# Gated-attention block: token halves of the MLP as even and odd chunks, their sums made in attention, both MLP stages laid out anew

## The chip, the cores and the metric

The kernel runs on one core of a Trainium2 chip, in one launch. The metric is device microseconds, the median of three timed runs. Beside them stands one execution taken by the hardware profiler, whose trace gives every row that is quoted here.

## The reference, cut to what matters

The input x is 2048 tokens of 1024 float32 values; a context of 256 tokens goes through the attention only. One layer is computed: a gated linear attention with a scan in both directions, then an MLP with squared ReLU, then a final RMS norm.

```python
a = modulate(rmsnorm(x, norm1_g), shift1, scale1)
o = gla_mixer(a_ctx, a)                        # scan over chunks, gate, output projection w_o
h = x + gate1 * o                              # h_d
h2 = modulate(rmsnorm(h, norm2_g), shift2, scale2)   # (2048, 1024)
m = square(relu(h2 @ mlp_w1)) @ mlp_w2         # 1024 -> 4096 -> 1024
out = rmsnorm(h + gate2 * m, final_g)
```

## The kernel before, in words

Matmuls run on float32r operands. So that the result keeps float32's precision, each operand is split into a high part (a ScalarE cast) and a low part (a subtraction), and `mm3` (lines 80 to 83) makes three matmuls of every one: high x high, high x low, low x high. A split is always such a pair, a cast and then a subtraction.

The kernel has four stages. (1) Up to about 889 us: projections and the scan (untouched by the change). (2) Up to about 1130 us, attention's second stage (lines 644 to 783): a loop over 16 chunks of 128 tokens. `front(ch)` finishes the scan's output, `turn_o` transposes it, `back(ch)` multiplies by w_o (48 matmuls of 512 columns), adds x, stores h to `h_d` and makes the normed rows hn. `turn(ch, hn)` (lines 747 to 770), called within the next chunk's `back`, transposes hn in eight blocks into two PSUM tiles, applies scale and shift while evicting them (half on ScalarE, L759, half on VectorE, L762) into `a2` (512 features x 128 tokens, float32), and stores that to `h2_d` (L764). For three of the four quarters of block 0 it also makes the split operands at once, into tiles of the pool `hold` (16 tiles of 4 KB a partition).

(3) The first MLP stage (lines 793 to 1001) computes square(relu(h2 @ w1)) in two blocks of 1024 tokens. It uses seven products in place of eight for a 2 x 2 blocked product (Strassen's scheme in Winograd's form). The token side has the quarters B11, B12, B21, B22 (first index: half of the 1024 features; second: half of the block's tokens, 512 each) and the sums T1 = B12 - B11, T2 = B22 - T1, T3 = B22 - B12, T4 = B21 - T2. The weight side has, for each of 16 pairs p of 128-column pieces of w1, A11 to A22 and the sums S1 to S4. The products are

```python
PROD = {1: ("a", "A11", "B11"), 5: ("b", "S1", "T1"), 6: ("a", "S2", "T2"), 2: ("c", "A12", "B21"),
        7: ("a", "S3", "T3"), 3: ("b", "S4", "B22"), 4: ("a", "A22", "T4")}
```

Each is 12 matmuls (4 k x `mm3`) of 512 columns. The letter names the PSUM accumulator, of which pool a has three banks, b three, c two. Products 1, 6, 7 and 4 of a pair add up in one bank; after product 1 its value is copied out (L967), after 6 too (L976), after 7 added to z22 (L981), after 4 evicted through ReLU (L985); bank b is copied after 5 (L973) and read after 3 (L978), bank c after 2 (L969). A matmul that goes on in a bank waits until the value was read. `order()` gives the order of products: for p >= 3 it is 1, 5, 6, 2, 7, 3, 4.

`load_h` (lines 815 to 850) loads a block's eight raw tiles from `h2_d` (L823), makes the sums (L804) and splits them (L808, L809, the subtractions on VectorE and GpSimd in turn) into the pool `m_t` of 18 tiles. For block 1 it is called at the last pair of block 0. `load_w1(p)` loads two raw tiles into `hold` (L864), makes S1 to S4 on VectorE and splits all seven operands (L857 the casts, L858 the subtractions: S1, S2, S4 and A11 on VectorE, S3, A12 and A22 on GpSimd). `sums_w2` makes sums of w2 for the last stage and stores them to `wt_d`. The seven hidden operands of each pair go to `hs_d` (L995).

(4) The second MLP stage (lines 1008 to 1124) does the same with w2: seven products, each over 16 pairs and two groups of 256 tokens; it loads `hs` tiles (L1025) and w2 tiles and splits them (L1030, L1031, L1040, L1041), and a product's result goes into `acc` and at the end to `out`. Output rows of token half 0 are the first 512 of a block, of half 1 the other 512.

What sets the order: the program is written down in order, and a planner fills each engine's queue from it, taking what it holds ready, in the order of priority. `tc.high_priority(offset=n)` gives instructions a priority as if they stood n instructions earlier. Each queue then runs in its order, and an instruction waits for the semaphores of what it needs. SyncE's queue (SP) issues nearly all DMAs. A pool with `reuse_waits="tile"` lets a new tile wait only for those older tiles that lay on its place; pools are stacked, so the order in which a stage opens its pools decides which tiles of the stage before lie there.

Of the kernel before, what the change touches and what calls it, by code (L numbers as in the profile page):

```python
# [8 lines left out]
F32 = mybir.dt.float32  # L9
# [4 lines left out]
ALU = mybir.AluOpType  # L14
# [23 lines left out]
def kernel(  # L38
# [34 lines left out]
    h2_d = dram.tile([P, ND, T], F32, name="h2_d")  # L73
# [561 lines left out]

    h2 = {}

    def h2_block(key):
        h2[key] = tuple(held([2, 512], F32R, "h2", 2) for _ in range(2))
# [4 lines left out]
    with ExitStack() as sb:  # L644
        wk = sb.enter_context(tc.tile_pool(name="b_wk", bufs=2, reuse_waits="tile"))
        wkx = sb.enter_context(tc.tile_pool(name="b_wkx", bufs=2, reuse_waits="tile"))
        wq = sb.enter_context(tc.tile_pool(name="b_q", bufs=2, reuse_waits="tile"))
        wk2 = sb.enter_context(tc.tile_pool(name="b_wk2", bufs=2, reuse_waits="tile"))
# [66 lines left out]
        def back(ch, onh, onl, hn_prev=None, mid=None, o_next=None):  # L715
            if ch == 0:
                h2_block((0, 0))
                h2_block((1, 0))
            elif ch == 4:
                h2_block((1, 1))  # L720
# [25 lines left out]

        def turn(ch, hn):
            for k4 in range(2):
# [4 lines left out]
                ks = slice(4 * k4, 4 * k4 + 4)  # L753
                t0 = (ch % 4) * P
                a2 = wk2.tile([P, 4, P], F32, tag="a2", name="a2", bufs=3)
# [8 lines left out]
                nc.sync.dma_start(h2_d[:, ks, ch * P:(ch + 1) * P], a2)  # L764
                if ch < MB // P and (k4, ch // 4) in h2:
                    for i in range(2):
                        dh, dl = (t_[i][:, :, t0:t0 + P] for t_ in h2[k4, ch // 4])
                        a_ = a2[:, 2 * i:2 * i + 2]
                        nc.scalar.copy(dh, a_)
                        nc.gpsimd.tensor_sub(dl, a_, dh.bitcast(F32))  # L770
# [8 lines left out]
        on = turn_o(nxt)  # L779
        for ch in range(1, NCH):  # L780
            nxt = front(ch + 1) if ch + 1 < NCH else None
            hn, on = back(ch, *on, hn, o_next=nxt)
# [10 lines left out]
    with ExitStack() as sm:  # L793
        tp = sm.enter_context(tc.tile_pool(name="m_t", bufs=18, reuse_waits="tile"))
        wp = sm.enter_context(tc.tile_pool(name="m_w", bufs=10, reuse_waits="tile"))
        cp = sm.enter_context(tc.tile_pool(name="m_c", bufs=2, reuse_waits="tile"))
        ev = sm.enter_context(tc.tile_pool(name="m_ev", bufs=12, reuse_waits="tile"))
# [3 lines left out]
        NK = ND // 2  # L801
# [4 lines left out]
        def split_h(src, alloc, eng):  # L806
            hi, lo = alloc(), alloc()
            nc.scalar.copy(hi, src)  # L808
            eng.tensor_sub(lo, src, hi.bitcast(F32))  # L809
            return hi, lo  # L810

        def t_tile(dtype=F32R, name="ht"):
            return tp.tile([P, 2, 512], dtype, tag="t", name=name)

        def load_h(b):
            r = {}
            for key in ((0, 0), (1, 0), (0, 1), (1, 1)):
                kh, th = key
                for j in range(2):
                    r[key, j] = t_tile(F32, "hraw")  # L820
                    k0 = NK * kh + 2 * j
                    t0 = b * MB + 512 * th
                    nc.sync.dma_start(r[key, j], h2_d[:, k0:k0 + 2, t0:t0 + 512])  # L823
            ops = {}

            def put(name, srcs, alloc, engs):
                hl = [split_h(s_, alloc, e_) for s_, e_ in zip(srcs, engs)]
                ops[name] = ([x_[0] for x_ in hl], [x_[1] for x_ in hl])
# [18 lines left out]
            if b > 0:  # L847
                put("B22", [r[(1, 1), j] for j in range(2)], hb, engs)
# [304 lines left out]
```

## Time and profile before

| | us |
|---|---|
| median of three runs | 2455.28 (2452.62 to 2456.47) |
| profiled execution | 2452.73 |
| its span, first to last instruction | 2451.0 |
| TensorE busy | 2303.0 |
| VectorE busy | 1580.3 |
| ScalarE busy | 1235.9 |
| GpSimd busy | 688.7 |

The span is what lies between the first and the last instruction of the profiled execution; the time of that execution has 1.7 us more. Busy time of an engine is the sum of its instructions without their overlap; matmuls overlap by their pipeline, so that a row's mean duration (390 ns) is longer than the spacing of two matmuls. Where a helper such as `mm3`, `tt` or a split makes every operation, the line number is the helper's and the tile names tell operations apart: pa, pb, pc are the first MLP stage's accumulators, yp attention's and the last stage's, pt the transposes, w1h and w1l split weights, ht or h split token operands, z and hs hidden values. Digits at the end of names are left out, so that `h2_d` stands as h_d.

### The profile page before, as it was taken

Reading aid. Unit: us, or ns where it says so; the run is one execution under the profiler, and the core shown is the slowest. Engines: PE = TensorE matmul, PEld = TensorE weight load, DVE = VectorE, ACT = ScalarE, POOL = GpSimd, SP = SyncE. Lnnn points to the kernel's source line nnn. Section 1 sums busy time; section 2 is a strip of 40 time slices with the busy share of each in tenths; the row PEclk is TensorE's granted clock in tenths of the full one; section 3 lists DMA queues with packets and bytes.
Section 4 is the critical chain, followed back from the end, with each engine's and each line's share of the span. In section 5 each row is a group of like instructions: output and inputs, shape, how many; then the busy total and the mean of one; then the engine's idle time right before and its main releaser. Section 6 shows DMA issues by size and latency. Waiting matters only on the chain. (4 is left out here: it accounts for less than half of the span.)

```text
span 2451.0 us, 36499 instructions
## 1 busy us (share of the span) xinstructions
PE 2303.0 (94%) x13250; PEld 2004.7 (82%) x13250; DVE 1580.3 (64%) x2287; ACT 1235.9 (50%) x2223; POOL 688.7 (28%) x765
## 2 busy tenths in 40 slices
PE   6899999999999989997899996999989999999998
PEld 4899999999999967785787884777768888888886
DVE  7855776676766677676866558665655448745484
ACT  6544544554555546554555554545554435444351
POOL 2334234434334434211322224222211113201021
PEclk8999999999999999998999998999999999999999
DMA  8223453444533277876466665666658657756572
GB/s 273 82 94 104 149 176 125 162 158 129 164 124 113 76 239 245 267 225 210 147 198 208 194 205 157 206 202 189 193 195 303 213 191 255 260 189 214 182 261 75
DMA packets 367934, 450.55 MB, mean 184 GB/s; under 512 B 22876, under 2 KB 273828, under 8 KB 367752
## 3 DMA queue, kind: packets, MB, share of 16 engines
q1 hardware_dynamic: 365080, 439.84, 54.8%
q0 software_dynamic: 2416, 8.07, 1.0%
q8 instruction: 104, 1.70, 0.3%
q14 instruction: 78, 0.64, 0.1%
q10 hardware_dynamic: 256, 0.29, 0.0%
HBM read 314.95 MB, written 133.17 MB: 183 GB/s over the span
## 5 line engine op out<-in xcount | busy, mean ns | idle before, releaser
L81 PE MATMUL yp<-w2h,hsh 128*128 128x512 f32 x896 | 349.7, 390 | 8.4 <-ACT hsh L1040 8.4
L83 PE MATMUL yp<-w2h,hsl 128*128 128x512 f32 x896 | 349.7, 390 | 0.1
L82 PE MATMUL yp<-w2l,hsh 128*128 128x512 f32 x896 | 349.5, 390 | 0.0
L342 POOL TENSOR_TENSOR wl<-wraw,wh 128x1024 fp32r<-128x1024 f32 x95 | 234.9, 2492 | 240.9 <-ACT wh L340 224.7
L858 POOL TENSOR_TENSOR w1l<-w1r,w1h 128x512 fp32r<-128x512 f32 x96 | 150.1, 1567 | 435.5 <-ACT w1h L857 290.3
L1041 DVE TENSOR_TENSOR hsl<-hsr,hsh 128x1024 fp32r<-128x1024 f32 x112 | 141.3, 1265 | 178.2 <-ACT hsh L1040 178.1
L1040 ACT CAST hsh<-hsr 128x1024 fp32r<-128x1024 f32 x112 | 117.7, 1052 | 204.1 <-PE yp L82 189.5
L1031 POOL TENSOR_TENSOR w2l<-w2r,w2h 128x512 fp32r<-128x512 f32 x56 | 81.5, 1456 | 462.0 <-ACT w2h L1030 358.4
L81 PEld LDWEIGHTS yp<-w2h,hsh 128*128 128x128 f32 x896 | 168.8, 188 | 43.9 <-ACT hsh L1040 8.9
L83 PEld LDWEIGHTS yp<-w2h,hsl 128*128 128x128 f32 x896 | 168.7, 188 | 35.9 <-DVE hsl L1041 0.8
L82 PEld LDWEIGHTS yp<-w2l,hsh 128*128 128x128 f32 x896 | 168.8, 188 | 35.1
L1030 ACT CAST w2h<-w2r 128x512 fp32r<-128x512 f32 x224 | 137.6, 620 | 93.1 <-PE yp L83 62.2
L81 PE MATMUL pa<-ht,w1h 128*128 128x512 f32 x384 | 154.3, 402 | 13.7 <-DVE z L981 7.4
L81 PE MATMUL vps<-wh,ah 128*128 128x256 f32 x576 | 165.1, 287 | 0.0
L82 PE MATMUL vps<-wl,ah 128*128 128x256 f32 x576 | 164.6, 286 | 0.0
L83 PE MATMUL vps<-wh,al 128*128 128x256 f32 x576 | 164.4, 285 | 0.0
L81 PE MATMUL kqps<-ah,wh 128*128 128x256 f32 x544 | 155.8, 286 | 0.0
L82 PE MATMUL kqps<-al,wh 128*128 128x256 f32 x544 | 154.8, 285 | 0.0
L83 PE MATMUL kqps<-ah,wl 128*128 128x256 f32 x544 | 154.1, 283 | 0.3 <-DVE wl L342 0.3
L82 PE MATMUL pa<-ht,w1h 128*128 128x512 f32 x384 | 150.4, 392 | 1.7 <-POOL ht L809 1.7
L83 PE MATMUL pa<-ht,w1l 128*128 128x512 f32 x384 | 149.7, 391 | 0.0
L82 PE MATMUL rps<-wl,ah 128*128 128x256 f32 x512 | 145.0, 283 | 0.0
(1278 smaller groups left out, 6498.1 us busy)
## 6 DMA issues: line engine op xcount, KB each, us to landing
hsr<-hs_d SPq DMA_DIRECT2D x112, 512.0 KB, 4.0
w2r<-in_mlp_w_dram SPq DMA_DIRECT2D x160, 256.0 KB, 4.1
wraw<-in_gla_w_in_dram SPq DMA_DIRECT2D x64, 512.0 KB, 3.8
w1r<-in_mlp_w_dram SPq DMA_DIRECT2D x64, 512.0 KB, 4.7
hs_d<-z SPq DMA_DIRECT2D x128, 256.0 KB, 2.8
w2r<-wt_d SPq DMA_DIRECT2D x128, 256.0 KB, 4.2
hs_d<-hs SPq DMA_DIRECT2D x96, 256.0 KB, 2.5
sp_d<-sp SPq DMA_DIRECT2D x60, 384.0 KB, 2.3
```

The lines of the kernel that those rows point to most:

```text
L81: nc.tensor.matmul(ps, sh, mh, start=start, stop=False, skip_group_check=skip)
L82: nc.tensor.matmul(ps, sh, ml, start=False, stop=False, skip_group_check=skip)
L83: nc.tensor.matmul(ps, sl, mh, start=False, stop=stop, skip_group_check=skip)
L342: eng.tensor_sub(wl[:, half * 4:half * 4 + 4, :], raw, hs.bitcast(F32))
L858: eng.tensor_sub(lo, src, hi.bitcast(F32))
L1030: nc.scalar.copy(hi, raw)
L1031: (nc.vector if f % 4 else nc.gpsimd).tensor_sub(lo, raw, hi.bitcast(F32))
L1040: nc.scalar.copy(hi, raw)
L1041: nc.vector.tensor_sub(lo, raw, hi.bitcast(F32))
```

## The change

Token half 0 of a block is now its even chunks and half 1 its odd chunks. So `turn` of an odd chunk has both halves at hand and makes T1 to T4 there; what it makes goes, by `give`, either into split tiles (block 0: B11, B21, T1) or to the new DRAM tensor `t_d`, seven operands per block. `load_t` loads one operand from it and splits it; there is no `load_h`. a2 lies in `hold`. The weight splits are made one by one, three products ahead, all on VectorE; raw weights are loaded seven products ahead, the first at the last chunk of attention. The operands of block 1 are loaded one by one, each when the last product of block 0 that uses it is placed. The order of products is new, and so are the pools of attention's second stage and both MLP stages. Output rows follow the chunks.

```diff
+    t_d = dram.tile([NB, NT, MB // P // 2, P, ND // 2, P], F32, name="t_d")
...
+    NCP = MB // P // 2
     def h2_block(key):
-        h2[key] = tuple(held([2, 512], F32R, "h2", 2) for _ in range(2))
+        h2[key] = tuple(held([NCP, 2, P], F32R, "h2", 2) for _ in range(2))
...
+        def give(b, cp, i, src):
+            if b == 0 and i in (IB11, IB21, IT1):
+                if cp == 0:
+                    h2_block(i)
+                for j in range(2):
+                    dh, dl = (t_[j][:, cp] for t_ in h2[i])
+                    nc.scalar.copy(dh, src[:, 2 * j:2 * j + 2])
+                    nc.gpsimd.tensor_sub(dl, src[:, 2 * j:2 * j + 2], dh.bitcast(F32))
+            else:
+                nc.sync.dma_start(t_d[b, i, cp], src)
+
         def turn(ch, hn):
+            b, cp = ch // (2 * NCP), ch // 2 % NCP
+            a_, = held([2, 4, P], F32, "a2", 1)
...
-                nc.sync.dma_start(h2_d[:, ks, ch * P:(ch + 1) * P], a2)
...
+                if ch % 2 == 0:
+                    give(b, cp, (IB11, IB21)[k4], a2)
+            if ch % 2 == 0:
+                even[0] = a_
+                return
+            e_ = even[0]
+            t1 = wkx.tile([P, 4, P], F32, tag="t1", name="t1", bufs=1)
+            nc.vector.tensor_sub(t1, a_[:, 0], e_[:, 0])
+            give(b, cp, IT1, t1)
+            nc.vector.tensor_sub(e_[:, 0], a_[:, 1], t1)
+            give(b, cp, IT2, e_[:, 0])
+            give(b, cp, IB22, a_[:, 1])
+            nc.vector.tensor_sub(a_[:, 0], a_[:, 1], a_[:, 0])
+            give(b, cp, IT3, a_[:, 0])
+            nc.vector.tensor_sub(e_[:, 1], e_[:, 1], e_[:, 0])
+            give(b, cp, IT4, e_[:, 1])
...
         for ch in range(1, NCH):
+            if ch == NCH - 1:
+                first_w.append(load_w1(0))
...
-        tp = sm.enter_context(tc.tile_pool(name="m_t", bufs=18, reuse_waits="tile"))
-        wp = sm.enter_context(tc.tile_pool(name="m_w", bufs=10, reuse_waits="tile"))
-        cp = sm.enter_context(tc.tile_pool(name="m_c", bufs=2, reuse_waits="tile"))
-        ev = sm.enter_context(tc.tile_pool(name="m_ev", bufs=12, reuse_waits="tile"))
+        ev = sm.enter_context(tc.tile_pool(name="m_ev", bufs=11, reuse_waits="tile"))
+        tl = sm.enter_context(tc.tile_pool(name="m_tl", bufs=4, reuse_waits="tile"))
+        tr = sm.enter_context(tc.tile_pool(name="m_tr", bufs=2, reuse_waits="tile"))
+        cp_ = sm.enter_context(tc.tile_pool(name="m_c", bufs=2, reuse_waits="tile"))
+        w1p = sm.enter_context(tc.tile_pool(name="m_w1", bufs=6, reuse_waits="tile"))
+        w2p = sm.enter_context(tc.tile_pool(name="m_w2", bufs=5, reuse_waits="tile"))
+        tp = sm.enter_context(tc.tile_pool(name="m_t", bufs=12, reuse_waits="tile"))
...
+        def load_t(b, i):
+            if b == 0 and i in h2:
+                return h2[i]
+            ops = ([], [])
             for j in range(2):
+                raw = tr.tile([P, NCP, 2, P], F32, tag="t", name="traw")
+                nc.sync.dma_start(raw, t_d[b, i, :, :, 2 * j:2 * j + 2].rearrange("c p k t -> p c k t"))
+                for n in range(2):
+                    if i in (IB11, IB21, IT1):
+                        t_, = held([NCP, 2, P], F32R, "h2", 1)
+                    else:
+                        t_ = (tl if i == IT2 else tp).tile([P, NCP, 2, P], F32R, tag="t", name="ht")
+                    if n == 0:
+                        nc.scalar.copy(t_, raw)
+                    else:
+                        nc.vector.tensor_sub(t_, raw, ops[0][j].bitcast(F32))
+                    ops[n].append(t_)
             return ops
...
+        def split_w(src, pool):
+            w_ = pool.tile([P, 2, NK, P], F32R, tag="w", name="w1")
+            nc.scalar.copy(w_[:, 0], src)
+            nc.vector.tensor_sub(w_[:, 1], src, w_[:, 0].bitcast(F32))
+            return w_[:, 0], w_[:, 1]
...
         def order():
+            two = lambda p, seq_: [(p + n, i) for i in seq_ for n in range(2)]
+            r = [(p, i) for p in range(2) for i in (1, 5, 2)] + two(0, (3, 6, 7))
+            late = [0, 1]
+            for p in range(2, NFP - 2):
+                r += [(p, 1), (p, 5)] + [(q, 4) for q in late] + [(p, 6), (p, 2), (p, 3), (p, 7)]
+                late = [p]
+            p = NFP - 2
+            return r + [(p, 1), (p, 5), (late[0], 4), (p + 1, 1), (p + 1, 5)] + two(p, (2, 6, 3, 7, 4))
...
+        def prepare(n):
+            while ahead[0] < len(seq_) and ahead[0] <= n + 7:
+                b, p, i = seq_[ahead[0]]
+                if (b, p) not in w1_ops:
+                    with tc.high_priority(offset=300):
+                        w1_ops[b, p] = first_w.pop() if (b, p) == (0, 0) else load_w1(p)
+                ahead[0] += 1
+            while ahead[1] < len(seq_) and ahead[1] <= n + 3:
+                b, p, i = seq_[ahead[1]]
+                with tc.high_priority(offset=400 if b == 0 and p < 2 else 100):
+                    get_w(w1_ops[b, p], PROD[i][1])
+                ahead[1] += 1
+            for b in range(NB):
+                for i in range(NT):
+                    if (b, i) not in t_ops and (b == 0 or n > last_use[b - 1, i]):
+                        with tc.high_priority(offset=100):
+                            t_ops[b, i] = load_t(b, i)
...
                 for k in range(NK):
-                    mm3(ps, ah[:, k], al[:, k], bh[k // 2][:, k % 2], bl[k // 2][:, k % 2], first and k == 0,
+                    mm3(ps_, ah[:, k], al[:, k], bh[k // 2][:, :, k % 2], bl[k // 2][:, :, k % 2], first and k == 0,
                         k == NK - 1, True)
...
-        acp = sm.enter_context(tc.tile_pool(name="n_acc", bufs=9, reuse_waits="tile"))
-        wp = sm.enter_context(tc.tile_pool(name="n_w", bufs=18, reuse_waits="tile"))
-        wr = sm.enter_context(tc.tile_pool(name="n_wr", bufs=6, reuse_waits="tile"))
-        hp = sm.enter_context(tc.tile_pool(name="n_h", bufs=6, reuse_waits="tile"))
-        hr = sm.enter_context(tc.tile_pool(name="n_hr", bufs=3, reuse_waits="tile"))
+        wp = sm.enter_context(tc.tile_pool(name="n_w", bufs=16, reuse_waits="tile"))
         xp = sm.enter_context(tc.tile_pool(name="n_x", bufs=2, reuse_waits="tile"))
         wk = sm.enter_context(tc.tile_pool(name="n_wk", bufs=2, reuse_waits="tile"))
+        wr = sm.enter_context(tc.tile_pool(name="n_wr", bufs=6, reuse_waits="tile"))
+        hr = sm.enter_context(tc.tile_pool(name="n_hr", bufs=3, reuse_waits="tile"))
+        acp = sm.enter_context(tc.tile_pool(name="n_acc", bufs=10, reuse_waits="tile"))
+        hp = sm.enter_context(tc.tile_pool(name="n_h", bufs=6, reuse_waits="tile"))
...
-                        row0 = b * MB + t * P
-                        row1 = row0 + 512
+                        row0 = b * MB + 2 * t * P
+                        row1 = row0 + P
```

`get_w` makes the sum that an operand needs and splits it with `split_w`, A11, S1 and A12 into `m_w1`, the others into `m_w2`. The pools of attention's second stage are opened in the order wkx, wk2, wk, wq, wo (before: wk, wkx, wq, wk2, wo).

## Rows read from the trace of the kernel before

**Rows 1.** Page, part 1: busy us, share of the span, instructions.
```profile
PE 2303.0 (94%) x13250; PEld 2004.7 (82%) x13250; DVE 1580.3 (64%) x2287; ACT 1235.9 (50%) x2223; POOL 688.7 (28%) x765
```

**Rows 2.** Table by stretch: window, its length, busy us and counts, clock, DMA share, GB/s.
```profile
889.00:1130.00 241.00, 224.91 (x1164) 184.52 (x1162) 170.05 (x350) 131.12 (x340) 65.24 (x99) 0.99 0.72 228
1129.93:1141.47 11.54, 2.13 (x10) 1.57 (x9) 6.06 (x13) 3.56 (x8) 0.74 (x2) 0.69 0.82 268
1141.47:1200.00 58.53, 44.07 (x161) 32.95 (x162) 53.65 (x49) 30.46 (x49) 25.65 (x13) 0.86 0.62 197
1200.00:1445.00 245.00, 240.92 (x1052) 195.95 (x1051) 148.43 (x210) 132.12 (x227) 59.39 (x38) 1.00 0.61 194
1445.00:1540.00 95.00, 73.78 (x298) 57.79 (x297) 71.74 (x75) 46.79 (x74) 34.66 (x18) 0.87 0.60 193
1540.00:1819.60 279.60, 272.43 (x1183) 220.15 (x1181) 163.49 (x228) 143.71 (x247) 61.35 (x39) 1.00 0.59 187
1819.60:1840.00 20.40, 11.87 (x40) 8.91 (x40) 14.81 (x17) 12.79 (x21) 6.79 (x4) 0.75 0.84 304
1840.00:2440.40 600.40, 600.40 (x2650) 497.17 (x2649) 343.96 (x375) 260.74 (x386) 100.87 (x95) 1.00 0.63 216
```

**Rows 3.** Waits of TensorE, 1140 to 1835: us in total, times, longest.
```profile
PE pa L81 <- ACT w1h L857: 21.2, 5, 12.3
...
PE pa L81 <- DVE z L981: 7.4, 8, 2.4
...
PE pa L81 <- ACT z L967: 5.9, 9, 1.3
```

**Rows 4.** Timeline of TensorE: start, us, instruction, [idle before, releaser].
```profile
1135.13 1.97 PE L752 MATMUL pt<-ident,hn 128*128 128x128 f32 x8 [5.04 <-DVE hn L744]
1141.47 0.79 PE L81 MATMUL pa<-h,w1h 128*128 128x512 f32 x1 [4.37 <-ACT w1h L857]
...
1485.15 0.80 PE L81 MATMUL pa<-h,w1h 128*128 128x512 f32 x1 [12.28 <-ACT w1h L857]
...
1828.26 0.80 PE L81 MATMUL yp<-w2h,hsh 128*128 128x512 f32 x1 [8.44 <-ACT hsh L1040]
```

**Rows 5.** Timeline of ScalarE at the start of the first MLP stage.
```profile
1139.23 0.46 ACT L759 ACTIVATE a<-pt,b,s 128x128 f32<-128x128 f32 x1 [0.48 <-DVE a L762]
1140.80 1.14 ACT L857 CAST w1h<-w1r 128x512 fp32r<-128x512 f32 x2 [1.11 <-DMA h_d<-a]
```

**Rows 6.** Page, part 6: DMA issues, count, KB each, us to landing.
```profile
w1r<-in_mlp_w_dram SPq DMA_DIRECT2D x64, 512.0 KB, 4.7
...
h_d<-a SPq DMA_DIRECT2D x32, 256.0 KB, 2.5
```

**Rows 7.** Groups of VectorE and of GpSimd, 1200 to 1445: busy us, mean ns.
```profile
L858 DVE TENSOR_TENSOR w1l<-w1r,w1h 128x512 fp32r<-128x512 f32 x12 | 8.2, 682 | 0.0
L858 DVE TENSOR_TENSOR w1l<-s__15544,w1h 128x512 fp32r<-128x512 f32 x3 | 3.2, 1058 | 0.0
...
L858 POOL TENSOR_TENSOR w1l<-w1r,w1h 128x512 fp32r<-128x512 f32 x38 | 59.5, 1569 | 189.2 <-ACT w1h L857 117.5 <-DVE hs L804 61.0 <-DVE z L981 9.4
```

**Rows 8.** Groups of VectorE and of ScalarE, 1200 to 1445: splits of 1024 elements.
```profile
L809 DVE TENSOR_TENSOR h<-hraw,h 128x1024 fp32r<-128x1024 f32 x1 | 1.2, 1225 | 1.1 <-POOL w1l L858 1.1
...
L808 ACT CAST h<-hraw 128x1024 fp32r<-128x1024 f32 x2 | 2.1, 1052 | 4.1 <-POOL w1l L858 4.1
```

**Rows 9.** Waits of TensorE in attention's second stage, 885 to 1140.
```profile
PE pt L710 <- ACT a L759: 10.8, 11, 2.8
```

**Rows 10.** Instructions of line 524 and of tile vps: ns min/median/max, first and last start.
```profile
L524 PE MATMUL pa<-qh,kh x256: 276/279/580, 90.5 to 853.3; 128*128 128x256 f32 x128
...
L81 PE MATMUL vps<-wh,ah x576: 277/283/415, 80.2 to 858.8; 128*128 128x256 f32 x192
```

**Rows 11.** Chain that ended last, at the hand-over: start, us, what.
```profile
1819.85 0.35 SPq L1025
...
1821.25 5.89 DMA hsr<-hs_d
```

More of the change, by code (lines that the diff above doesn't have):

```diff
@@ L72 @@
     h_d = dram.tile([T, D], F32, name="h_d")
-    h2_d = dram.tile([P, ND, T], F32, name="h2_d")
+    NT = 7
+    IB11, IB21, IT1, IT2, IB22, IT3, IT4 = range(NT)
+    t_d = dram.tile([NB, NT, MB // P // 2, P, ND // 2, P], F32, name="t_d")
     hs_d = dram.tile([NB, 7, 2, P, NFP, 256], F32, name="hs_d")
@@ L715, in back @@
         def back(ch, onh, onl, hn_prev=None, mid=None, o_next=None):
[L716 to L720, printed above, removed]
             on = None
@@ new lines, in split_w, with get_w @@
+        def split_w(src, pool):
[3 more added lines that the diff above has]
+            return w_[:, 0], w_[:, 1]
+        def get_w(ops, name):
+            if name not in ops:
+                a11, a12, a21, a22 = ops["raw"]
+                if name == "S1":
+                    ops["s"] = cp_.tile([P, NK, P], F32, name="s_")
+                    tt(nc.vector, ops["s"], a21, a22, ALU.add)
+                elif name == "S2":
+                    tt(nc.vector, ops["s"], ops["s"], a11, ALU.subtract)
+                elif name == "S4":
+                    get_w(ops, "S2")
+                    tt(nc.vector, ops["s"], a12, ops["s"], ALU.subtract)
+                elif name == "S3":
+                    tt(nc.vector, a21, a11, a21, ALU.subtract)
+                ops[name] = split_w({"A11": a11, "A12": a12, "A22": a22, "S3": a21}.get(name, ops.get("s")),
+                                    w1p if name in ("A11", "S1", "A12") else w2p)
+            return ops[name]
@@ L923, in ev_tile @@
             return ev.tile([P, 512], F32, tag="ev", name=name)
-        w1_ops = {}
-        def get_w1(b, p, offset):
-            if (b, p) not in w1_ops:
-                with tc.high_priority(offset=offset):
-                    w1_ops[b, p] = load_w1(p)
-        for p in range(PRO):
-            get_w1(0, p, 200)
-        def block(b):
-            if b == 0:
-                hops = load_h(b)
-            else:
-                hops = hops_next.pop()
-            st = {}
-            for p, i in order():
-                if p not in st:
-                    st[p] = {}
-                    get_w1(b, p, 300)
-                    if p + 1 < NFP and p >= PRO:
-                        pass
+        seq_ = [(b, p, i) for b in range(NB) for p, i in order()]
+        w1_raw, w1_ops, t_ops = {}, {}, {}
+        ahead = [0, 0]
+        last_use = {}
+        for n, (b, p, i) in enumerate(seq_):
+            last_use[b, PROD[i][2]] = n
+        def prepare(n):
[15 more added lines that the diff above has]
+                            t_ops[b, i] = load_t(b, i)
+        st = {}
+        for n, (b, p, i) in enumerate(seq_):
+            prepare(n)
+            if True:
+                if (b, p) not in st:
+                    st[b, p] = {}
                     if p % 2 == 0:
                         sums_w2(b * (NFP // 2) + p // 2)
-                    if b + 1 < NB and p == NFP - 1:
-                        with tc.high_priority(offset=300):
-                            hops_next.append(load_h(b + 1))
-                s = st[p]
+                s = st[b, p]
                 bank, an, bn = PROD[i]
```

151 lines of the change are left out of this document (32 added, 119 removed).

## The prediction

> **What bounds the kernel now.** I read the page first: TensorE is busy 94% of the span, VectorE 64%, GpSimd 28% [rows 1]. So the sum is over time in which TensorE has no work or runs slowly, and the question is in which stage that time lies. The table by stretch answers it [rows 2]. Its last row is the yardstick: in the second MLP stage 2650 matmuls of 512 columns stand in 600.4 us without a gap, 0.2266 us each. Both MLP stages have 2688 such matmuls (two blocks, 16 pairs, 7 products, 4 x 3), and the change leaves their number alone. What a stretch loses is its length less its count times 0.2266 [rows 2]:
>
> - start of the first MLP stage, 1129.93 to 1200: 11.54 less 1.97 for the last eight transposes [rows 4] is 9.6, and 58.53 - 161 x 0.2266 = 22.0; together 31.6 us
> - steady, 1200 to 1445 and 1540 to 1819.6: 245 - 1052 x 0.2266 = 6.6, and 279.6 - 1183 x 0.2266 = 11.5; together 18.1 us
> - change of block, 1445 to 1540: 95 - 298 x 0.2266 = 27.5 us
> - hand-over to the second MLP stage, 1819.6 to 1840: 20.4 - 40 x 0.2266 = 11.3 us
>
> That is 88.5 us, all around the first MLP stage. The second stage has nothing to give, and the scan ahead of 889 us isn't touched. Who ends these waits stands in the list of waits: 21.2 us for the cast of a w1 operand, 7.4 us for the add of product 7 (L981), 5.9 us for the copy of product 1 (L967) [rows 3]. The timeline of TensorE puts single gaps in place: 5.04 us for hn, 4.37 us at the first product, 12.28 us in the change of block, 8.44 us at the hand-over [rows 4].
>
> **Start (31.6 us; I forecast 17).** Before, the first product waits at 1141.47 for the cast of A11, and that cast for the landing of the last h2_d store, at 1140.80 [rows 5]: the weight tiles lie where attention's tiles lay. After, w1's raw tiles for pair 0 are asked for at the last chunk, their split tiles lie over tiles that attention has left by then, and products 1, 5 and 2 of pair 0 use B11, T1 and B21, which are already split in SBUF. These 36 matmuls (8.2 us) can run from 1129.93, under the wait for hn and with the 2.0 us of transposes, to 1140.1. What is late next is pair 1. The `hold` pool has 16 tiles: 12 for B11, B21 and T1, two for w1 of pair 0, two for the last two chunks' a2. So w1 of pair 1 can't be loaded before the stores of T1 to T4 of the last chunk have landed. Last a2 piece at 1139.7 [rows 5], three to four subtractions of 0.69 us, 2.5 us for the store and 4.7 us for w1 [rows 6], cast and subtraction 0.6 + 0.7: about 1150.5, a gap of 10.4 us. The hand-over shows what such a gap costs beside itself: 11.3 less 8.44, about 3 us at a lower clock [rows 2, 4]. For the other operands, which pass through two raw buffers, I add 3.6: 17. Bounds: 5, if pair 0's later products fill the gap, and 31.6, no gain.
>
> **Steady (18.1; I forecast 6).** The accumulator of bank a is read between products 1 and 6 and between 7 and 4; in the old order one product (2.7 us) covers each of these reads, in the new one two (5 and the late 4; 1 and 5 of the next pair). The waits are 7.4 + 5.9 us in all [rows 3], about 2.4 of them in the start; I drop the remaining 11 and keep 6 to 7. Against this stands VectorE: the three splits of each pair that GpSimd made go to it. Between 1200 and 1445 it is busy 148.4 of 245 us [rows 2], and GpSimd makes 38 splits there [rows 7]; at 0.68 us each [rows 7] that is 26 us more, 174 of 245 (71%). I take the plain sum. It fits, so it costs nothing as long as it is only work; its queueing is what keeps me at 6 and not at 2. Bounds: 0 and 20.
>
> The same rows show a VectorE split at 1.06 us in one place and 0.68 in another, and GpSimd's at 1.57 [rows 7]. The Trainium skill (SBUF — State Buffer, "Who interferes with whom") says that a VectorE instruction with two SBUF inputs contends with a GpSimd instruction that reads SBUF. By that rule the splits lose this lengthening when GpSimd stops, some 0.37 us each, and VectorE would stand nearer 65% than 71%. It speaks against the change too: in attention the new subtractions would meet GpSimd's own. No term of the sum hangs on it.
>
> **Change of block (27.5; I forecast 8).** Before, all eight raw tiles of the next block come at once, and sums and splits of seven operands stand in VectorE, ScalarE and GpSimd in front of the weights. After, the sums are read ready-made, and an operand is reloaded as soon as its last product is done: B11 is free after the fourth of the block's last 15 products and wanted 11 products later; the last, T4, is wanted 25 products (25 x 12 x 0.2266 = 68 us) after B11 came free. In these 68 us VectorE has 14 splits of 1024 elements at 1.2 us [rows 8], 17 us, beside 68 x 174/245 = 48 us of its own: 65 of 68. ScalarE has 14 x 1.05 = 15 us [rows 8] beside 68 x 132/245 = 37 [rows 2]. It fits, but barely; a queue so full makes evictions late. I take 8. Bounds: 0 and 27.5. The loads (14 x 512 KB) have 30 us of lead each. On SP a load that waits for one of the two raw buffers holds up what is queued behind it, w1's loads and the stores of hs, and for w1 the next pair's casts wait; with 30 us of lead I cost that at nothing, and in the second rival it is part of what is lost. GpSimd's queue only loses work.
>
> **Hand-over (11.3; I forecast 2).** Before, the load of the first hs tile is issued at 1819.85, when the last matmul has ended, and takes 5.89 us [rows 11]: its buffer lies on an operand in use. In the new layout the raw buffers lie on T2's tiles, free six products (16 us) before the end, the w2 tiles on `hold`, and the first split hs tile on weights that are done three products earlier. Load and cast then lie under matmuls. Bounds: 0 and 11.3. The w2 pool of 16 instead of 18 costs nothing: a tile is freed 20 us before its next use, and a load, cast and subtraction take some 6.
>
> **Attention's second stage (+2).** Each odd chunk adds four VectorE subtractions of 512 elements: 8 x 4 x 0.69 = 22 us on an engine busy 170 of 241 us [rows 2], so 80%. TensorE's largest repeated wait there is for ScalarE's evictions of the transposes, 10.8 us in 11 waits [rows 9], which VectorE's queue can lengthen. Stores: four per two chunks as before in block 0, seven instead of four in block 1, 256 KB each, in 2 KB runs instead of 512 B. I take +2; bounds -3 (the split of T and the stores get lighter) and +10 (as much again as that wait).
>
> **The matmul's moving operand** becomes four runs of 128 columns. The nearest row is L524, two runs of 128: 279 ns against 283 for the contiguous vps [rows 10]. I take 0; bounds -2 and +2 ns, 5 us either way.
>
> **Sum.** 14.6 + 12.1 + 19.5 + 9.3 - 2 = 53.5 us off the profiled execution, 2452.73 (span 2451.0 and 1.7 around it): 2399.2. The median of the three runs is 2.55 above the profiled one, so 2401.8, rounded to 2401.
>
> **Rivals.**
>
> - All waits go. Start 6, steady 3, change 1, hand-over 0, attention 0: 88.5 - 10 = 78.5 less, 2377. For it: every part has slack on paper. Against it: pair 1's wait for `hold`. Chance 0.17; 2368 to 2386.
> - The order doesn't come out as written. A planner fills each engine's queue by what it holds ready; if the first three products stay behind the last transposes, or T's splits push the weights' aside, start keeps 28 and change 20: 3.6 + 7.5 + 12.1 + 9.3 - 2 = 30.5 less, 2425. For it: VectorE at 65 of 68. Against it: both stretches still lose the summing. Chance 0.20; 2416 to 2445.
> - Slower: VectorE becomes the bound of the first MLP stage. Its 20 operations a pair are 20 x 0.69 = 13.8 us, T's splits 1.1, in 19.0 us (84 x 0.2266). Each split waits for its cast, so the engine can stand idle with work queued; if that takes a pair to 22 us, 32 x 3 = 96 us are added to the floor of 2364 + 2.5 with 15 of start and hand-over left: 2477. It is slower from 21.4 us a pair on. Against it: 13.8 + 1.1 us of work would have to hold the engine for 21.4. Chance 0.05.
> - Slower: the four runs cost time. 20 ns a matmul give the whole gain back (2688 x 0.020 = 54), 25 make 2468. Against it: L524. Chance 0.04.
> - No change: gains and new waits cancel, 2450 to 2460. Chance 0.04.
>
> **How the numbers follow.** The forecast, 2386 to 2416 by its own range, has 0.50. Faster by over 0.2% (about what the runs can tell from no change, 5 us): 0.50 + 0.17 + 0.20 = 0.87; the same 0.04; slower 0.09. The range from 2374 to 2440 takes in the forecast, two thirds of the first rival and nearly all of the second, about 0.80.
>
> **What would show it.** Right: matmuls of pc or pb before 1140, ahead of or between the last transposes; a gap of about 10 us before pair 1's product 1, ended by a w1 cast; no gap over 3 us between 1445 and 1540; no TensorE wait on L967 and L981's successors in the steady part; the first yp matmul within 2 us of the last pa matmul. Wrong: a spacing of more than 0.23 us in the first MLP stage; VectorE over 90% there; TensorE waits in attention above 15 us for ScalarE's evictions.

## The result, and the profile after

The changed kernel takes 2411.68 us (median of four runs, 2410.83 to 2416.79) against 2454.32 us for the kernel before in the same series: a ratio of 0.983, 95% interval 0.9813 to 0.9847. The forecast was 2401, range 2374 to 2440, so the direction and the range hold, and the time is 10.7 us above the forecast. The profiled execution took 2412.02 us, with a span of 2410.3.

Page, part 1, of the kernel after (answers to [rows 1]):

```profile
PE 2312.0 (96%) x13250; PEld 2008.1 (83%) x13250; DVE 1603.7 (67%) x2410; ACT 1239.1 (51%) x2223; POOL 524.1 (22%) x658
```

Table by stretch of the kernel after (columns as in [rows 2]; the bounds are moved to where its stages lie):

```profile
1138.20:1200.00 61.80, 53.40 (x226) 42.21 (x225) 54.08 (x82) 37.97 (x63) 1.41 (x2) 0.94 0.90 288
1200.00:1445.00 245.00, 245.00 (x1083) 202.93 (x1082) 164.55 (x251) 140.67 (x232) 0.00 (x0) 1.00 0.68 214
1445.00:1540.00 95.00, 91.43 (x395) 74.56 (x394) 76.08 (x117) 60.09 (x100) 0.00 (x0) 0.98 0.78 250
1540.00:1766.20 226.20, 226.20 (x999) 187.09 (x997) 143.75 (x221) 126.86 (x214) 3.91 (x3) 1.00 0.63 205
1766.20:1790.00 23.80, 20.43 (x76) 15.80 (x76) 17.35 (x21) 12.68 (x17) 1.82 (x1) 0.86 0.94 321
1790.00:2399.60 609.60, 609.60 (x2614) 491.16 (x2613) 347.81 (x368) 252.92 (x380) 114.65 (x94) 1.00 0.59 205
```

The terms come from it by the prediction's own method, a stretch less its count times 0.2266. Start: 61.8 - 226 x 0.2266 and 1.0 for the last transposes. Attention: its last matmul by w_o ended at 1129.9 before and at 1138.1 after.

| | lost before | forecast | lost after | forecast gain | measured gain |
|---|---|---|---|---|---|
| start | 31.6 | 17 | 9.6 | 14.6 | 22.0 |
| steady | 18.1 | 6 | 0 | 12.1 | 18.1 |
| change of block | 27.5 | 8 | 5.5 | 19.5 | 22.0 |
| hand-over | 11.3 | 2 | 6.6 | 9.3 | 4.7 |
| attention | | | | -2 | -8.2 |
| second MLP stage | | | | 0 | -17.2 |
| sum | | | | 53.5 | 41.4 |

The spans differ by 40.7. The last line is the one that the prediction has no term for: the last stretch has no gap, at granted clock 1.00, but 609.6 / 2614 = 0.2332 us a matmul in place of the 0.2266 of [rows 2]. 2614 x 0.0066 = 17.2 us.

Waits of TensorE in the kernel after, 1140 to 1800 (answers to [rows 3]):

```profile
PE pb L84 <- ACT w L863: 5.5, 1, 5.5
PE yp L84 <- ACT hs L1039: 2.2, 1, 2.2
PE pb L84 <- ACT z L977: 1.9, 1, 1.9
PE pa L84 <- DVE z L980: 1.7, 1, 1.7
PE pa L84 <- DVE z L986: 1.7, 1, 1.7
PE yp L86 <- DVE hs L1040: 1.2, 1, 1.2
```

The casts of w1 operands have fallen from 21.2 to 5.5 us, in one gap, and the waits for z from 13.3 to 5.3 in three. Timeline of TensorE, the gaps of the start and the change of block (answers to [rows 4]):

```profile
1142.75 1.09 PE L776 MATMUL pt<-ident,hn 128*128 128x128 f32 x8 [0.17 <-DVE hn L752]
1157.99 0.79 PE L84 MATMUL pb<-h,w 128*128 128x512 f32 x1 [5.51 <-ACT w L863]
...
1451.92 0.50 PE L84 MATMUL pa<-ht,w 128*128 128x512 f32 x1 [1.67 <-DVE z L986]
1481.34 0.50 PE L84 MATMUL pb<-ht,w 128*128 128x512 f32 x1 [1.90 <-ACT z L977]
```

### The profile page after: what moved, and what is told of

The parts are those of the page before. It is cut to its first block, busy times and chain, and to the rows that moved or that the text cites. A ratio compares the mean times of both kernels' runs of the same rounds, so it can differ in the third digit from the quotient of the medians.

```text
span 2410.3 us, 36228 instructions
## 1 busy us (share of the span) xinstructions
PE 2312.0 (96%) x13250; PEld 2008.1 (83%) x13250; DVE 1603.7 (67%) x2410; ACT 1239.1 (51%) x2223; POOL 524.1 (22%) x658
## 4 chain that ended last, share of the span: by engine, by line
PE 49%; DVE 4%; issue 4%; DMA 3%; POOL 1%; ACT 1%; SPq 0%; POOLq 0%; DVEq 0%; ACTq 0%
PE yp L86 9%; PE yp L85 9%; PE yp L84 9%; PE pa L84 4%; PE pa L85 4%; PE pa L86 4%; PE pb L84 2%; PE pb L85 2%; PE pb L86 2%; DMA uu<-sp_d 1%; PE pc L84 1%; PE pc L85 1%; PE pc L86 1%; DMA w2r<-in_mlp_w_dram 1%; DMA traw<-t_d 1%
## 5 line engine op out<-in xcount | busy, mean ns | idle before, releaser
L84 PE MATMUL yp<-w,hs 128*128 128x512 f32 x896 | 355.4, 397 | 2.2 <-ACT hs L1039 2.2
L86 PE MATMUL yp<-w,hs 128*128 128x512 f32 x896 | 355.5, 397 | 1.2 <-DVE hs L1040 1.2
L85 PE MATMUL yp<-w,hs 128*128 128x512 f32 x896 | 355.4, 397 | 0.0
L1031 POOL TENSOR_TENSOR w<-w2r,w 128x512 fp32r<-128x512 f32 x56 | 98.7, 1763 | 1052.9 <-ACT w L1030 1052.6
L1040 DVE TENSOR_TENSOR hs<-hsr,hs 128x1024 fp32r<-128x1024 f32 x112 | 140.0, 1253 | 145.1 <-ACT hs L1039 140.8
L1039 ACT CAST hs<-hsr 128x1024 fp32r<-128x1024 f32 x112 | 117.3, 1049 | 202.0 <-PE yp L86 143.2
L84 PEld LDWEIGHTS yp<-w,hs 128*128 128x128 f32 x896 | 169.0, 189 | 43.4 <-ACT hs L1039 2.6
L86 PEld LDWEIGHTS yp<-w,hs 128*128 128x128 f32 x896 | 169.1, 189 | 42.5 <-DVE hs L1040 1.7
L85 PEld LDWEIGHTS yp<-w,hs 128*128 128x128 f32 x896 | 169.0, 189 | 40.8
L1030 ACT CAST w<-w2r 128x512 fp32r<-128x512 f32 x224 | 137.6, 620 | 112.8 <-PE yp L86 103.5
L1031 DVE TENSOR_TENSOR w<-w2r,w 128x512 fp32r<-128x512 f32 x168 | 135.5, 820 | 63.4 <-ACT w L1030 62.0
L84 PE MATMUL pa<-ht,w 128*128 128x512 f32 x384 | 149.7, 390 | 3.4 <-DVE z L980 1.7
L85 PE MATMUL pa<-ht,w 128*128 128x512 f32 x384 | 149.4, 389 | 0.0
L86 PE MATMUL pa<-ht,w 128*128 128x512 f32 x384 | 149.4, 389 | 0.0
```

Of the source, the lines that this page charges most:

```text
L84: nc.tensor.matmul(ps, sh, mh, start=start, stop=False, skip_group_check=skip)
L85: nc.tensor.matmul(ps, sh, ml, start=False, stop=False, skip_group_check=skip)
L86: nc.tensor.matmul(ps, sl, mh, start=False, stop=stop, skip_group_check=skip)
L1030: nc.scalar.copy(w_[:, 0], raw)
L1031: (nc.vector if f % 4 else nc.gpsimd).tensor_sub(w_[:, 1], raw, w_[:, 0].bitcast(F32))
L1039: nc.scalar.copy(h_[:, 0], raw)
```

## The experiments

Two questions were open: what slows the second MLP stage, whose instructions did not change in number, and where attention's 8 us come from. Beside them, which part of the change made the steady stretch free of waits. Times are medians; a ratio is to the kernel before, run in the same series, with its 95% interval.

**The second stage.** Its tiles lie differently. The change opens its pools in the order n_w, n_x, n_wk, n_wr, n_hr, n_acc, n_h. In bytes a partition all but n_wk are multiples of 512; n_wk holds ten small tiles of 32 bytes beside 6144 of larger ones, so the stationary hs tiles lie 320 bytes off a multiple of 512 from the moving w2 tiles. Before, n_wk came last and the distance was a multiple of 512. The first guess was that 128 bytes are what counts.

e1, two more of the small tiles (distance 384):

```diff
-ssq = wk.tile([P, 3], F32, tag="ssq", name="ssq", bufs=6)
+ssq = wk.tile([P, 3], F32, tag="ssq", name="ssq", bufs=8)    # in both places
```

> The changed kernel with two more of the small ssq tiles, so that the stationary hs tiles of the second MLP stage lie a multiple of 128 bytes from the moving w2 tiles, as they did before, instead of 64 bytes off it. Nothing else moves. Theory A (the distance of the two operands' addresses modulo 128 bytes costs 6 to 7 ns a matmul of 512 columns): 2688 x 0.0066 = 17.7 us less, about 2394, the spacing in the second MLP stage back at 0.2266 us. Rival B (the spacing comes from something else that the change brought into that stage, the hi and lo parts joined in one tile or a fuller ScalarE): no change, 2410 to 2414, spacing 0.233.

2411.82 us, 0.9834 (0.9809 to 0.986): no change, so the guess fell in this form. Rival B had the number right; its cause (the joined tiles) fell with e5 below, which keeps them. Table by stretch of e1, 600 / 2584 = 0.2322 us each:

```profile
1790.00:2390.00 600.00, 600.00 (x2584) 486.51 (x2583) 349.16 (x368) 253.30 (x382) 114.41 (x94) 1.00 0.62 210
```

e2, the kernel before with its hs tiles moved by 64 bytes:

```diff
+pd = sm.enter_context(tc.tile_pool(name="n_pd", bufs=1, reuse_waits="tile"))
+nc.gpsimd.memset(pd.tile([P, 16], F32, name="pad"), 0.0)
 hp = sm.enter_context(tc.tile_pool(name="n_h", bufs=6, reuse_waits="tile"))
```

> The kernel before with one unused tile of 64 bytes a partition ahead of the hs tiles of its last stage, so that these lie 64 bytes off a multiple of 128 from the w2 tiles; hi and lo parts are in separate tiles here. Theory A (address distance): 17 to 18 us more, about 2472, spacing in the second MLP stage 0.233 in place of 0.2266. Rival B (the joined tiles of the change): no change, 2453 to 2456.

1.0144 (1.012 to 1.0167), 2489 us. That is 34 us more, twice what theory A said. No spacings are read from e2; e7 below takes the 34 us apart.

e1 left a finer reading. The long runs at 0.2267 us in both kernels, in both MLP stages, have tiles that differ by a multiple of 512. So three more pads, ahead of n_h as in e2's diff: 48 floats (192 bytes) and 112 floats (448) in the changed kernel, 128 floats (512) in the kernel before.

> The changed kernel with one unused tile of 192 bytes a partition ahead of the hs tiles of the second MLP stage. The trace of e1 showed that a multiple of 128 bytes is not enough: its spacing stayed at 0.232. In the traces so far all long runs of matmuls at 0.2267 us have stationary and moving tiles whose addresses differ by a multiple of 512 bytes; in the second MLP stage of the changed kernel they differ by 320 (modulo 512), in e1 by 384. Here the difference is 0 modulo 512. Theory A (512 bytes is what counts): spacing 0.2267 after the first ten or so matmuls, 17 to 18 us less, about 2394. Rival B (the joined hi and lo tiles, or a state that is fallen into by chance at the hand-over): 2409 to 2416, spacing 0.232 to 0.233.

> The same with 448 bytes in place of 192, so that the addresses differ by 256 modulo 512. Theory A (512): spacing 0.232 to 0.2335, about 2410. Rival (256 is enough): spacing 0.2267, about 2394.

> The kernel before with 512 unused bytes ahead of its hs tiles in place of the 64 of e2: the addresses differ by 0 modulo 512 again, while the hs tiles are moved onto later neighbours as in e2. e2 took 2489, 34 us more than before. Theory A: half of that is the spacing and half a later first cast at the hand-over (the hs tile lies on one more operand), so about 2471 here, spacing 0.2267. Rival B (address distance does nothing; e2's loss is all at the hand-over): about 2489.

e5: 2397.23, 0.976 (0.9745 to 0.9774). e6: 2399.77, one run. e7: 2472.86, 1.0068 (1.0048 to 1.0088). Tables by stretch of the three, in this order:

```profile
1790.00:2380.00 590.00, 590.00 (x2605) 488.54 (x2604) 352.71 (x369) 254.52 (x383) 115.52 (x94) 1.00 0.63 217
```

```profile
1790.00:2380.00 590.00, 590.00 (x2604) 488.54 (x2604) 352.75 (x369) 253.34 (x383) 112.46 (x94) 1.00 0.63 217
```

```profile
1870.00:2450.00 580.00, 580.00 (x2561) 480.41 (x2560) 332.01 (x365) 253.66 (x378) 96.41 (x93) 1.00 0.63 211
```

All three stand at 0.2265 us. Theory A's spacing holds for e5 and e7, and their times came out 3 and 2 us above its numbers. In e6 it was wrong in its number and the rival right: 256 bytes are enough. e2 less e7 is 16 us, the spacing's part of e2. The rest is the hand-over, where e7's TensorE waits 25.9 us for the first hs cast instead of 8.44 (17.5 more; e7 is 17.2 above the kernel before):

```profile
PE yp L81 <- ACT hsh L1042: 25.9, 1, 25.9
```

Is that peculiar to the second stage? e11 takes e5 and shifts the first stage's weights by 64 bytes. Four products have token operands that stay where they were; those of the other three move along with the weights:

```diff
+pm = sm.enter_context(tc.tile_pool(name="m_pd", bufs=1, reuse_waits="tile"))
+nc.gpsimd.memset(pm.tile([P, 16], F32, name="pad1"), 0.0)
 w1p = sm.enter_context(tc.tile_pool(name="m_w1", bufs=6, reuse_waits="tile"))
```

> Kernel e5 (2397) with 64 unused bytes ahead of the split weights of the first MLP stage. Products 1, 2, 5 and 6 (1536 matmuls) then have weights that lie 64 bytes off a multiple of 256 from their token operands; products 3, 7 and 4 (1152 matmuls) move with their weights and stay at a multiple of 256, as does the whole second stage. Theory A (the distance of the two tiles sets the spacing, in any stage): products 1, 2, 5 and 6 at 0.232 to 0.2335, the others at 0.2267 after a few matmuls, 1536 x 0.0066 = 10 us more, about 2407. Rival B (it is peculiar to the second stage and its moving operand in one run): 2394 to 2400, spacing 0.2267 throughout.

2405.76, 0.9817 (0.9801 to 0.9833), 8.5 us over e5; theory A. The two profiled executions differ less (2401.14 and 2400.57), since attention ended 7 us earlier in e11's; from its first to its last matmul, the first MLP stage took 636.6 us in e11 and 630.1 in e5. The spacing, from the starts of neighbouring matmuls between 1200 and 1760, is 233.1 to 233.3 ns in products 1, 5, 2 and 6, and 226.9 in product 7, which uses the same bank as 6; in products 3 and 4 it is 228.4 and 228.3, where the first few after a product of the other kind are still long. The weights of all seven were moved by 64 bytes, so it is the distance of the two tiles that counts, and not the address of the weights. The same shows in the durations. Groups of TensorE, 1200 to 1445, e11 and then e5 (busy, mean ns):

```profile
L84 PE MATMUL pa<-h,w 128*128 128x512 f32 x52 | 20.5, 394 | 0.0
L84 PE MATMUL pb<-h,w 128*128 128x512 f32 x52 | 20.5, 394 | 0.0
L84 PE MATMUL pc<-h,w 128*128 128x512 f32 x52 | 20.5, 394 | 0.0
```

```profile
L84 PE MATMUL pc<-h,w 128*128 128x512 f32 x56 | 21.8, 389 | 0.0
L84 PE MATMUL pa<-h,w 128*128 128x512 f32 x52 | 20.2, 389 | 0.0
L84 PE MATMUL pb<-h,w 128*128 128x512 f32 x52 | 20.2, 389 | 0.0
```

**Attention.** The end of the stage alone is a poor measure, since what comes ahead of it varies: the hundredth of its 768 matmuls by w_o started between 924 and 931 us. From the hundredth to the last it is steadier: 205.4 and 206.3 us in the two profiles with the old attention (before, e7), 211.5 to 213.1 in seven profiles with the new one (after, e1, e3, e5, e6, e9, e11). So the change costs some 7 us there. e8 leaves the four subtractions out:

```diff
-nc.vector.tensor_sub(t1, a_[:, 0], e_[:, 0])
-give(b, cp, IT1, t1)
+give(b, cp, IT1, a_[:, 0])
...                                            # and so for T2, T3 and T4
```

> The changed kernel without the four VectorE subtractions of each odd chunk; the plain pieces are stored and split in the place of T1 to T4, so the products use other operands than they should. Everything else of the change stays: stores, splits, layouts. Theory A (attention's 8 us are these subtractions in VectorE's queue): 6 to 9 us less, 2403 to 2406, and the waits for st and onl fall to 1 us or less. Rival B (the stores of seven operands, the held a2 tiles or the splits of T1 cost it): under 2 us less, 2410 to 2413.

2402.75, 0.978 (0.9753 to 0.9807): 8.9 less, as theory A has it. Its sign came in part: the waits for onl are gone, and those for st fell from 6.3 to 2.3 us and not to 1. Waits of TensorE in e8, 889 to 1145:

```profile
PE pov L85 <- DVE st L701: 2.3, 3, 1.7
```

e4 puts the subtractions on GpSimd:

```diff
+te = nc.vector if ch == NCH - 1 else nc.gpsimd
-nc.vector.tensor_sub(t1, a_[:, 0], e_[:, 0])
+te.tensor_sub(t1, a_[:, 0], e_[:, 0])        # all four
```

> The changed kernel with the four subtractions that make T1 to T4 on GpSimd, except for the last chunk. Theory A (attention lost 8 us because these 22 us of work stand in VectorE's queue ahead of the adds and splits that TensorE waits for): the 6.3 us of waits for st and the 2.9 us for onl go, 4 to 8 us less, 2404 to 2408. Rival B (GpSimd's subtractions slow VectorE's own instructions as its splits did before, and take more than twice as long themselves): no gain or a loss, 2411 to 2420, with VectorE's subtractions over 0.8 us in that stage.

2440.91, 0.9948 (0.9934 to 0.9961): 29 us more, on rival B's side and beyond its range. Its sign did not show: VectorE's subtractions for onl (L725) took 0.69 us as after, and only the splits of st (L701) lengthened, from 0.48 to 0.61. The tables of that stretch, before, after, e8 and e4:

```profile
924.26:1129.93 205.67, 197.69 (x1035) 163.73 (x1033) 140.94 (x301) 111.55 (x294) 52.46 (x85) 1.00 0.72 229
```

```profile
925.12:1138.10 212.98, 201.79 (x1035) 165.14 (x1034) 161.54 (x327) 113.92 (x297) 55.13 (x85) 0.99 0.68 230
```

```profile
927.11:1127.84 200.73, 197.13 (x1035) 163.78 (x1034) 141.55 (x299) 112.58 (x297) 51.61 (x85) 1.00 0.74 243
```

```profile
931.10:1171.20 240.10, 212.34 (x1035) 174.08 (x1034) 149.79 (x299) 113.51 (x297) 89.11 (x113) 0.94 0.61 203
```

The number of TensorE instructions is the same in all four. The subtractions cost 12.3 us (212.98 less 200.73), for 20.0 us of VectorE's time (161.54 less 141.55); without them the new attention would be 5 us faster than the old. Why is GpSimd worse? Several waits grow in e4. Waits of TensorE in e4, 889 to 1170, and of VectorE, 908 to 1170:

```profile
PE pt L723 <- ACT a L781: 23.0, 12, 3.8
PE pov L85 <- DVE st L701: 10.2, 13, 1.7
```

```profile
DVE o L712 <- POOL rsr L95: 29.4, 14, 4.7
```

VectorE waited 29.4 us for GpSimd's rsr (the power of the norm, L95) against 23.6 after: GpSimd's queue also holds 28 subtractions of 1.28 to 1.42 us. The larger wait is ScalarE's, for the load of rr. Waits of ScalarE, 908 to 1170 in e4 and 908 to 1140 after:

```profile
ACT rr L692 <- DMA rr<-sp_d: 28.4, 6, 5.6
```

```profile
ACT rr L692 <- DMA rr<-sp_d: 1.4, 5, 0.4
```

SyncE's queue in e4 shows why that load is late. It stands behind the stores of what the subtractions make, and there each store waits for its subtraction; the four take 6.76 us, where they take 1.8 after:

```profile
1017.14 6.76 SPq L767 DMA_DIRECT2D t_d<-a  x4
1023.95 0.53 SPq L691 DMA_DIRECT2D rr<-sp_d  x1
```

The transposes waited 23.0 us for ScalarE's evictions against 3.9. No run separates the two chains.

**The steady part.** e3 puts the old order of products back, e9 the splits of A12, A22 and S3 onto GpSimd:

```diff
-r += [(p, 1), (p, 5)] + [(q, 4) for q in late] + [(p, 6), (p, 2), (p, 3), (p, 7)]
+r += [(p, 1), (p, 5)] + [(q, 4) for q in late] + [(p, 6), (p, 2), (p, 7), (p, 3), (p, 4)]
-late = [p]
+late = []
```

> The changed kernel with the old order of products in the steady part (..., 6, 2, 7, 3, 4 with no late 4): one product instead of two between those that share a bank. Theory A (the second covering product took the waits for the eviction away): the waits for z come back, 8 to 18 us more over the steady part (the 18.1 us lost there before as the upper end), 2420 to 2430. Rival B (the waits came from VectorE splits that GpSimd's own splits lengthened from 0.69 to over 1 us, and are gone because GpSimd makes none now): under 3 us more, 2411 to 2415.

```diff
-nc.vector.tensor_sub(w_[:, 1], src, w_[:, 0].bitcast(F32))
+eng.tensor_sub(w_[:, 1], src, w_[:, 0].bitcast(F32))   # nc.gpsimd for S3, A12, A22
```

> The changed kernel with the subtractions of the splits of A12, A22 and S3 on GpSimd again, as before the change; the new order of products stays. e3 put the old order back and lost 8 us, so some 10 of the 18 us that the steady part lost before are not told by the order. Theory A (they were these splits: GpSimd took 1.57 us for one and lengthened VectorE's from 0.68 to over 1 us): 5 to 12 us more, 2417 to 2424, with VectorE's splits over 0.9 us between 1200 and 1445. Rival B (with two products of cover a late split reaches no matmul): under 3 us more, 2411 to 2415, though VectorE's splits lengthen.

e3: 2419.7, 0.9855 (0.9831 to 0.988), 8 us more. e9: 2420.78, 0.9863 (0.9837 to 0.9889), 9 us more. The times sit at or close to where both theories A put them, though both intervals overlap that of the change (0.9813 to 0.9847), and the traces carry the theories only in part. Table by stretch, e3 and then e9:

```profile
1200.00:1445.00 245.00, 243.92 (x1071) 200.02 (x1070) 166.88 (x253) 135.73 (x229) 0.00 (x0) 1.00 0.66 210
...
1540.00:1760.00 220.00, 219.26 (x962) 179.59 (x961) 141.71 (x217) 116.81 (x201) 0.00 (x0) 1.00 0.61 198
```

```profile
1200.00:1445.00 245.00, 242.38 (x1066) 199.52 (x1065) 149.12 (x223) 132.60 (x227) 46.03 (x35) 1.00 0.68 214
...
1540.00:1760.00 220.00, 220.00 (x971) 181.82 (x970) 124.33 (x189) 119.08 (x205) 44.88 (x34) 1.00 0.64 205
```

By counts e3 loses 2.3 + 2.0 us in these stretches and e9 3.4 + 0. The kernel before loses 18.1 in its steady part. e9's expectation of VectorE splits over 0.9 us failed too: they took 0.782 us, against 0.689 after, while GpSimd's took 1.315. Each half alone keeps most of the gain. That the rest comes back only when both are undone was not run. Nor does any run undo the third novelty, that the splits are made one by one and three products ahead. What made most of the gain stays open.

**A version that beats both.** e8 said that VectorE's queue is what attention is short of, so e10 takes e5 and moves one more thing out of it:

```diff
-nc.vector.tensor_scalar(hn, xt, r2[:, 0:1], None, op0=ALU.mult)
+nc.scalar.mul(hn, xt, r2[:, 0:1])
```

> Kernel e5 (2397) with the scaling of hn in attention, 16 instructions of 0.75 us, on ScalarE in place of VectorE. e8 showed that VectorE's queue is what attention lost. Theory A (any 12 us less in that queue help as the subtractions did, in proportion 12 to 26): 3 to 5 us less, 2392 to 2394. Rival B (hn's scaling is on the path to the transposes and ScalarE, which also makes the casts and half of the evictions, takes longer for it): 2397 to 2402, with more wait of the transposes for ScalarE.

2391.53, 0.9741 (0.972 to 0.9762). That is 5.7 less than e5, a little more than theory A, and 20 less than the change. Its interval overlaps that of e5, but the trace agrees: from the hundredth to the last matmul by w_o it takes 207.5 us, and e5 213.1. Rival B's sign did not show: the transposes waited 5.0 us for ScalarE, 6.1 in e5. The stretch of e10 that answers to the four above:

```profile
928.88:1136.50 207.62, 199.49 (x1035) 163.39 (x1034) 147.06 (x313) 127.58 (x311) 59.49 (x85) 1.00 0.71 236
```

## Why the prediction was right, and where it was not

The four terms around the first MLP stage were 55.5 us together and came out at 66.8. The sizes of three of them were timid. The trace shows the mechanism of the start and of the change of block, which no run takes apart; that of the steady part is shown for a small share only.

*Start.* The chain that the prediction wrote is there: the stores of T, then pair 1's w1, then its cast. SyncE's queue after:

```profile
1144.51 0.37 SPq L651 DMA_DIRECT2D w1r<-in_mlp_w_dram  x1
1146.46 0.33 SPq L767 DMA_DIRECT2D t_d<-t  x1
1148.00 1.80 SPq L767 DMA_DIRECT2D t_d<-a  x4
...
1151.48 1.73 SPq L651 DMA_DIRECT2D w1r<-in_mlp_w_dram  x2
```

The gap it makes is 5.51 us where 10.4 was forecast, and it stands ahead of pair 1's product 5 (pb), not of its product 1. The prediction had both raw tiles of pair 1 wait for the stores. One of them took the place of a raw tile of pair 0 once its last sum (L840) was made, and was asked for at 1144.51, ahead of the stores, so that pair 1's product 1 ran from 1149.17 and covered part of the chain. Attention's later end covers some of it too: the products of pair 0 run until 1149 and not until 1140. Product 1 of pair 0 started directly behind the last matmul of attention, at 1138.20, ahead of the last transposes.

*Steady.* The 6 us kept for VectorE's queueing were not needed: 1083 matmuls in 245 us is no loss at all, with VectorE at 164.6 us (67%), under the 71% of the plain sum. What made the steady part free of waits is another question. The prediction put it to the order, two products in place of one between those that share a bank; with the old order back, e3 loses 4.3 us where the kernel before lost 18.1. So the term came out without its mechanism being shown for most of it. The plain sum took 0.68 us for a split and left VectorE's other work as it was. Its splits of raw tiles took 0.689 us as forecast, and the longer ones of [rows 7] have gone with GpSimd's. The Trainium skill (SBUF — State Buffer, "Who interferes with whom") says that a VectorE instruction with two SBUF inputs contends with a GpSimd instruction that reads SBUF; by that rule the prediction had VectorE nearer 65% than 71%, and 67% agrees. In attention it shows from the other side. Two of the four subtractions after the change: the group of T1 in 908 to 1140, and that of T3 over the whole span (shortest, median and longest ns):

```profile
L793 DVE TENSOR_TENSOR t<-a,a 128x512 f32<-128x512 f32 x7 | 4.8, 688 | 0.2 <-ACT a L781 0.2
```

```profile
L798 DVE TENSOR_TENSOR a<-a x8: 684/958/1235, 936.9 to 1147.9; 128x512 f32<-128x512 f32 x8
```

Each T is one subtraction of the same size; L795 makes T2 and L800 T4. T1 and T2 take 0.69 us throughout. T3 and T4 take 1.23 us in the four odd chunks of block 0, where GpSimd splits T1 at that time, and 0.69 in the four of block 1, where it splits nothing.

*Change of block.* 65 of 68 us looked barely enough; two gaps of 1.67 and 1.90 us are all that is left, and 5.5 us with their tails.

*Hand-over, the first step that failed.* The forecast was that load and cast lie under matmuls. The load does: it was issued at 1751.20. The operands under the first hs tile are done three products before the end, at about 1758. But its cast stands behind casts of w2 and evictions of z on ScalarE and is made at 1767.52, after the last product's end at 1766.2:

```profile
1765.35 1.12 ACT L1030 CAST w<-w2r 128x512 fp32r<-128x512 f32 x2
1766.37 0.58 ACT L990 ACTIVATE z<-pa 128x512 f32<-128x512 f32 x1
1766.99 0.63 ACT L991 ACTIVATE z<-z 128x512 f32<-128x512 f32 x1
1767.52 2.92 ACT L1039 CAST hs<-hsr 128x1024 fp32r<-128x1024 f32 x3
```

I followed the tile and the load, and not the queue of the engine that casts. The gaps are 2.22 and 1.16 us, and the matmuls behind them run at the lower of the two clock levels: their spacing is 427 ns until 1775.5, and the granted clock of 1766.2 to 1790 is 0.86. That another order of the casts would mend it was not run.

*Attention, mis-sized.* +2 was forecast, within -3 to +10, and the stretch that can be compared gives +7.3, of which the subtractions are 12.3 and everything else -5. What in the rest makes it faster was not separated. The prediction named 22 us of work on VectorE and a lighter split, but looked for the cost at the evictions of the transposes. These waits fell, from 10.8 us [rows 9] to 3.9, and new ones came. Waits of TensorE after, 880 to 1140:

```profile
PE pov L85 <- DVE st L701: 6.3, 9, 1.0
PE pt L723 <- ACT a L781: 3.9, 7, 0.9
...
PE yp L86 <- DVE onl L725: 2.9, 5, 0.6
```

80% busy was not spare time: VectorE makes st and onl for TensorE, and four subtractions in a row are 2.7 us (block 1) or 3.8 us (block 0) in front of them.

*Second stage, the largest miss.* "The second stage has nothing to give" was read as "nothing to lose". Its pools were laid out anew in the diff, and the prediction asked of them only which operands lie beneath. With e5's pad the change takes 2397, 4 us under the forecast. That the total came so near is in part luck: by the table the second stage (17.2), attention (6.2) and the hand-over (4.6) missed by 28.0 us on one side, and the start (7.4), the steady part (6.0) and the change of block (2.5) by 15.9 on the other.

The rivals: VectorE did not become the bound, the four runs cost nothing (pa, pb and pc in four runs of 128 columns stand at 226.7 ns from start to start between 1200 and 1445), and the order came out as written but for small swaps (product 2 of pair 0 ran ahead of its product 5).

## What to carry to other kernels

When a change lays pools out anew, work out the address of each matmul's two operands modulo 256 bytes, and pad small tiles so that the difference is 0; it cost 3% of every matmul of a stage here, with no wait and no gap to show it. An engine with idle time that makes another engine's operands is not free for that reason. In attention, where VectorE is busy for 76% of the time, 20.0 us of added work cost 12.3 us; in the first MLP stage, at 67%, it took over GpSimd's splits at no cost. So look at what stands behind the added work in the engine's queue. And follow a step that is to be hidden through all three: the buffer, the load, and the queue of the engine that handles it next.

## What the hardware showed that was not expected

The mean spacing of 512-column matmuls from start to start, without gaps and at granted clock 1.00, by the distance of the stationary from the moving tile modulo 256 bytes (other distances were not run):

| distance | spacing, ns | where |
|---|---|---|
| 0 | 226.7 | first stage before and after, second stage before and of e5, e6, e7 |
| 64 | 233.3 | second stage after, products 1, 5, 2 and 6 of e11's first stage |
| 128 | 232.4 | second stage of e1 |

At distance 0 a run of matmuls that starts behind a wait also has some 5 to 11 long spacings (224 to 236 ns), and then settles at 226.7; in the second stages after and of e1 it never does, over some 2600 matmuls. The cause was not isolated. The Trainium skill (TensorE: Matmul & The Clock Gate, "Step-by-step: what each phase is for") says that the streaming operand and the weight load have independent SBUF read ports, so that loading the next weights takes no read bandwidth from the running matmul. These runs show something beside it: the two overlap here (weight loads are busy for 491.2 of the 609.6 us of the second stage after, under matmuls without a gap), and where their tiles lie relative to each other changes the spacing by 6 to 7 ns. That the two reads meet in the memory is the nearest reading, and no run shows it.
